# The last down projection of a two-layer trunk by seven products over K pairs

## The chip, the cores and the metric

The kernel runs on one core of one Trainium2 chip as one launch. Its time is the device time in microseconds of that core. The time before is the median of three runs. The profile is one further execution of the same program, recorded by the profiler; its span runs from the first to the last instruction.

## The reference, cut to what matters

A trunk of two layers over 1024 prompt frames and 32 sample frames, model width 1024, in float32. Layer 0 has a retention mixer, layer 1 a gated linear attention; after each mixer comes a ConvFFN of width 2816, and at the end one RMS norm. The change lies in the ConvFFN of layer 1 and the final norm.

```python
def conv_ffn(h, conv_state, w_up, conv_w, conv_b, w_down):
    u = h @ w_up
    ...
    gate, val = jnp.split(c, 2, axis=-1)
    return (jax.nn.silu(gate) * val) @ w_down, ext[:, T:]

def trunk(...):
    for i in range(DEPTH):
        ...
        h = rmsnorm(x, norm_ffn[i])
        y, cs = conv_ffn(h, conv_states[i], ffn_w_up[i], ffn_conv_w[i], ffn_conv_b[i], ffn_w_down[i])
        x = x + y
    return rmsnorm(x, norm_final), ...
```

## The kernel before

Activations lie transposed: 128 features in the partitions, the 1056 frames (prompt and sample) in the columns. To keep float32 accuracy with the fp32r form that TensorE takes, each operand is split into a high part (a cast by ScalarE) and a low part (a subtraction by VectorE), and each product is three matmuls: high x high, high x low, low x high. PE is TensorE, DVE VectorE, ACT ScalarE, POOL GpSimd, SP the engine that issues most transfers.

**The up projection** (`ffn_up` with `seven`) already uses seven products in place of eight: the 1024 input features are halved, the two output tiles of one f (its gate tile and its value tile) are one side of a 2 x 2 block product, and pairs of column quarters of 264 columns the other. `ORD = (1, 2, 6, 5, 7, 4, 3)` is the order of the products, s (0 or 1) is the column half. Each product is four K tiles x three matmuls of 264 columns (L436, L440, L441). Three PSUM banks, a, b and c, hold the sums of one (f, s): products 1, 6 and 7 build up in a, 2 and later 4 use b, 5 and 3 build up in c. After products 1, 6 and 7 ACT copies the bank (`snap`, L415); after 2, 7, 4 and 3 DVE adds copy and bank into the row buffer u (`put`, L1607). Sums of weights are made on DVE (L373, L387 and neighbours). There are ten weight tiles in a ring, of which one f takes seven, so the last tiles for f + 1 come free only with the last products of f. The stage runs over 22 f; the sequence of the products of both halves is written out in `seq`, with s = 1 three and a half products behind s = 0.

After the last product of an f, `conv(f)` applies the causal convolution (per half one ACT pass, L1633, and two DVE passes, L1634 and L1635, over 1058 columns), silu on ACT (L213), the product of gate and value on DVE (L1638), and two stores of the row h into `scr_h` in DRAM.

**The last down projection** is a `Down` of 22 K tiles. It goes over the columns in three chunks (384, 384 and 288). For each chunk and K tile the weight tile w_down (128 x 1024) is loaded and split (L110), unless it was kept from the chunk before, the rows of h are loaded and split (L1483, L1484), and 8 x 3 matmuls (L1519, L1520, L1521) add into eight PSUM banks, one for each output tile. At the end of a chunk DVE adds each bank to the residual row (L1881), ACT squares it and scales it by the norm's weight. `rms_row` (L231 to L250) sums the squares over partitions with a matmul by ones and makes the inverse root (Ln, Exp, and one correction step). The scaled rows (L1902) are stored to `o_y`. For the first two chunks norm and scaling run beside the matmuls of the next chunk; for the third they follow the last matmul.

The order of the instructions on each engine is laid down at build time by a planner that takes what is ready, older instructions first; each engine then runs its queue in that order. `order(a, b)` puts a behind b. Tile pools make an instruction wait for the release of its buffer.

Buffers that the change touches: `XA`, `XB` and `XH` hold the split inputs of the up projection (28 areas of 4 x 264 columns), `AR` the rows u and c and the residual, `HR` the copies.

## Time and profile before

| | |
|---|---|
| median of 3 runs | 2813.46 us (2811.8 to 2814.3) |
| profiled execution | 2813.36 us, its span 2811.6 us, granted clock 0.998 |
| last up projection | about 2093 to 2544 us of the span |
| last down projection | 2544 to 2800.5 us |
| last matmul of it to the end of the span | 11.1 us |
| all DMA over the span | 371.10 MB, mean 132 GB/s |

Lines of the profile read as line of code, engine, operation, what is written from what, count, then busy time in us and the mean of one in ns, then the idle time of that engine just before and what ended it. PE's busy time comes from overlapping instructions: a matmul of 264 columns is listed with 284 ns, but the next one begins after less than half of that, so stages are compared by count and length, not by the sum of durations.

### The profile page before, as it was taken

The page shows a single profiled execution, that of the slowest core. Times are in us where ns is not written, and L with a number is a line of the kernel's source. Part 1 is how long each engine was busy: PE and PEld are TensorE (multiplying, and loading weights), DVE is VectorE, ACT ScalarE, POOL GpSimd, SP SyncE. Part 2 cuts the span into 40 slices and gives each one's busy share as a digit, 9 for nine tenths or more (in the row PEclk, how much of TensorE's full clock was granted, in tenths as well). Part 3 has the DMA queues.
Part 4 walks back from the last instruction along what each step waited for, and adds up shares of the span by engine and source line. Part 5 has one row for each costly group of instructions (what it writes and reads, how often), then busy time and mean ns, then how long its engine had stood idle before and what let it go on. Part 6 is the DMA issues. An engine that isn't in the chain of part 4 may idle for free.

```text
span 2811.6 us, 53490 instructions
## 1 busy us (share of the span) xinstructions
PE 2781.7 (99%) x21692; PEld 2695.0 (96%) x21692; DVE 1904.8 (68%) x3214; ACT 1337.6 (48%) x2409; POOL 311.3 (11%) x576
## 2 busy tenths in 40 slices
PE   9999999999999999999999999999999999999998
PEld 9999988888999999999999999999999999999998
DVE  7876666676457877777555576775378777775545
ACT  7544354454445444444444466653354444444444
POOL 0000000000122211111000032210132111110000
PEclk9999999999999999999999999999999999999999
DMA  6333455554875222222755501116532222227544
GB/s 239 94 113 100 148 148 151 139 150 124 284 240 182 77 84 77 78 82 84 264 185 168 168 30 53 53 45 212 187 108 80 73 85 76 84 75 253 190 150 148
DMA packets 220472, 371.10 MB, mean 132 GB/s; under 512 B 60672, under 2 KB 155008, under 8 KB 216896
## 3 DMA queue, kind: packets, MB, share of 16 engines
q1 hardware_dynamic: 212928, 330.36, 36.9%
q0 software_dynamic: 6736, 36.72, 3.9%
q8 instruction: 170, 2.79, 0.4%
q14 instruction: 78, 0.64, 0.1%
q10 hardware_dynamic: 560, 0.59, 0.1%
HBM read 275.68 MB, written 91.93 MB: 131 GB/s over the span
## 4 chain that ended last, share of the span: by engine, by line
PE 84%; DVE 7%; ACT 3%; POOL 2%; issue 2%; DMA 1%; SPq 0%; DVEq 0%; ACTq 0%; POOLq 0%
PE pu L441 13%; PE pu L436 13%; PE pu L440 13%; PE pd L1519 8%; PE pd L1521 8%; PE pd L1520 8%; PE psv L270 2%; PE psv L271 2%; PE psv L272 2%; POOL x L1122 2%; PE pg L133 1%; PE pg L134 1%; PE pg L135 1%; PE pj L885 1%; DMA raw<-w_ro 1%
## 5 line engine op out<-in xcount | busy, mean ns | idle before, releaser
L110 DVE TENSOR_TENSOR wlo<-raw,whi 128x1024 fp32r<-128x1024 f32 x188 | 234.5, 1250 | 221.6 <-ACT whi L110 211.1
L110 ACT CAST whi<-raw 128x1024 fp32r<-128x1024 f32 x188 | 196.9, 1050 | 282.1 <-PE pd L1520 210.0
L1519 PE MATMUL pd<-hh,whi 128*128 128x384 f32 (+1 forms) x880 | 285.0, 324 | 0.0
L1520 PE MATMUL pd<-hl,whi 128*128 128x384 f32 (+1 forms) x880 | 284.3, 323 | 0.1
L1521 PE MATMUL pd<-hh,wlo 128*128 128x384 f32 (+1 forms) x880 | 283.9, 323 | 0.0
L415 ACT COPY HR<-pu 128x264 f32<-128x264 f32 x264 | 98.7, 375 | 311.8 <-PE pu L441 305.5
L441 PE MATMUL pu<-XA,wgl 128*128 128x264 f32 x752 | 213.4, 284 | 0.0
L436 PE MATMUL pu<-XA,wgh 128*128 128x264 f32 x752 | 212.8, 283 | 0.0
L440 PE MATMUL pu<-XA,wgh 128*128 128x264 f32 x752 | 212.5, 283 | 0.0
L1520 PEld LDWEIGHTS pd<-hl,whi 128*128 128x128 f32 x880 | 165.7, 188 | 0.9 <-DVE hl L1484 0.4
L1634 DVE SCALAR_TENSOR_TENSOR AR<-AR,cw 128x1058 f32<-128x1058 f32 x88 | 115.8, 1318 | 74.7 <-ACT AR L1633 74.6
L1519 PEld LDWEIGHTS pd<-hh,whi 128*128 128x128 f32 x880 | 165.7, 188 | 0.4
L1521 PEld LDWEIGHTS pd<-hh,wlo 128*128 128x128 f32 x880 | 165.7, 188 | 0.1
L373 DVE TENSOR_TENSOR wtl<-rv,wth 128x1024 fp32r<-128x1024 f32 x58 | 71.0, 1224 | 113.5 <-ACT wth L372 113.4
L1607 DVE TENSOR_TENSOR AR<-HR,pu 128x264 f32<-128x264 f32 (+2 forms) x440 | 144.3, 368 | 4.6 <-PE pu L441 4.6
L436 PEld LDWEIGHTS pu<-XA,wgh 128*128 128x128 f32 x752 | 141.2, 188 | 0.3 <-ACT wgh L372 0.3
L440 PEld LDWEIGHTS pu<-XA,wgh 128*128 128x128 f32 x752 | 141.2, 188 | 0.0
L441 PEld LDWEIGHTS pu<-XA,wgl 128*128 128x128 f32 x752 | 141.1, 188 | 0.0
L436 PE MATMUL pu<-XA,wsh 128*128 128x264 f32 x464 | 132.6, 286 | 2.4 <-ACT HR L415 1.3
L441 PE MATMUL pu<-XA,wtl 128*128 128x264 f32 x464 | 131.9, 284 | 0.0
L441 PE MATMUL pu<-XA,wsl 128*128 128x264 f32 x464 | 131.8, 284 | 0.0
L436 PE MATMUL pu<-XA,wth 128*128 128x264 f32 x464 | 131.6, 284 | 0.0
(503 smaller groups left out, 9625.1 us busy)
## 6 DMA issues: line engine op xcount, KB each, us to landing
raw<-w_down SPq DMA_DIRECT2D x120, 512.0 KB, 3.7
rg<-w_up SPq DMA_DIRECT2D x44, 512.0 KB, 3.6
rv<-w_up SPq DMA_DIRECT2D x44, 512.0 KB, 3.6
scr_h<-AR SPq DMA_DIRECT2D x44, 512.0 KB, 2.6
raw<-w_ro SPq DMA_DIRECT2D x39, 512.0 KB, 5.7
XH<-scr_hr POOLq DMA_DIRECT2D x16, 1056.0 KB, 7.1
HR<-scr_h SPq DMA_DIRECT2D x84, 192.0 KB, 3.9
scr_hr<-hl SPq DMA_DIRECT2D x20, 512.0 KB, 4.2
```

The source lines that it names most:

```text
L110: ins = S.copy(hi, raw), V.tensor_tensor(lo, raw, hi.bitcast(F32), op=ALU.subtract)
L270: PE.matmul(ps, ah, hi, start=kt == 0, stop=False)
L373: split_end[0] = split_last[0] = V.tensor_tensor(l_, src, h.bitcast(F32), op=ALU.subtract)
L415: ins = S.copy(t, b)
L436: mm = PE.matmul(ps, wh[:, k], x[:, 0, kt], start=m in (1, 2, 4, 5) and kt == 0, stop=False, skip_group_check=True)
L440: PE.matmul(ps, wh[:, k], x[:, 1, kt], start=False, stop=False, skip_group_check=True)
L441: mm = PE.matmul(ps, wl[:, k], x[:, 0, kt], start=False, stop=kt == 3, skip_group_check=True)
L1519: PE.matmul(o, w[0][:, k], h[0][:, :n], start=i == 0, stop=False)
L1520: PE.matmul(o, w[0][:, k], h[1][:, :n], start=False, stop=False)
L1521: self.last_mm = PE.matmul(o, w[1][:, k], h[0][:, :n], start=False, stop=i == nk - 1)
L1607: last_put[0] = V.tensor_tensor(u[:, d:d + n], t[:, o:o + n], b[:, o:o + n], op=op)
L1634: V.scalar_tensor_tensor(cj, uj[:, 1:T + 3], cw[:, nt, 1:2], cj, op0=ALU.mult, op1=ALU.add)
```

## The change

It replaces the three chunks of the last down projection by the seven-product form. The 22 K tiles become 11 pairs, the 8 output tiles 4 pairs, the columns two halves s of two quarters each.

- `pair_sums`, in place of L1638 and the two stores: after the convolution of an odd f the product rows of both f of a pair are combined into the seven right-hand operands (four subtractions of 528 columns, in two steps that are called at later products), and the seven are stored to `scr_h7`, each when it is made.
- `Down7` runs over 14 windows n. Window n holds the K pairs n - 3 to n, so one to four of them (`win`), and the output pair (n + 1) % 4. Every K pair so meets each of the four output pairs in four successive windows. Per window there are seven products for each s, of one to four K pairs x three matmuls of 264 columns, s = 0 and s = 1 in turn. The weights of a window are loaded as two tiles, combined and split as in the up projection (`weights`). The operands of a K pair are loaded and split once (`load_x`); four K pairs stay in `XA`, `XB` and `XH`.
- In windows 0 to 9 the bank sums go by ACT and DVE into blocks in `AR` and `HR` (five for the first output tile, two for the second), and POOL adds each block to the residual in `scr_x` by an adding transfer (`add`).
- The last four windows (10 to 13, output pairs 3, 0, 1, 2) complete an output pair each: the row pair with all that was added is fetched (`fetch`) and the banks are added into it (`settle`). `squares` gathers the sums of squares; with the last pair each quarter's norm is made and all four pairs are scaled and stored.
- `early` brings the first two K pairs and the weights of windows 0 and 1 in during the last f of the up projection. `final_phase` goes. `HR` is one area larger.

```diff
-    def ffn_up(l, X, fc, sm):
+    NP = NF // 2
+    class Down7:
...
+            self.win = [list(range(max(0, n - 3), min(n, NP - 1) + 1)) for n in range(NP + 3)]
...
+            self.blocks = [[HR[:, o * b:o * b + b] for o in range(3)] + [AR[:, o * b:o * b + b] for o in (8, 9)],
+                           [AR[:, o * b:o * b + b] for o in (10, 11)]]
+            self.SS = [HR[:, s * b:s * b + b] for s in range(2)]
+            self.sq = [HR[:, 4 * TH + j * TH:5 * TH + j * TH] for j in range(3)]
+            self.nsq = 0

+        def load_x(self, k, i, n=1):
+            reg, j = self.at[7 * (k % 4) + i]
+            v = reg[:, j * 4 * TH:(j + n) * 4 * TH].rearrange("p (m j u) -> p m j u", m=n, j=2)
+            hi, lo, raw = v[:, :, 0], v[:, :, 1], v[:, :, 1].bitcast(F32)
+            nc.sync.dma_start(raw, io["scr_h7"][k, :, i:i + n].rearrange("p m s t -> p m (s t)"))
+            for m in range(n):
+                self.X[k, ORD[i + m]] = v[:, m].rearrange("p j (s t) -> p j s t", s=2)
+            def split():
+                S.copy(hi, raw)
+                V.tensor_tensor(lo, raw, hi.bitcast(F32), op=ALU.subtract)
+            return split
+        def weights(self, n):
+            h = len(self.win[n]) * P
+            a, b = slice(0, h), slice(h, 2 * h)
+            rg, rv = raw_tile(f"dg{uid()}"), raw_tile(f"dv{uid()}")
+            for j, r in enumerate((rg, rv)):
+                o = self.offs[n] + j * 2 * h * P
+                nc.sync.dma_start(r[:, :2 * h], io["w_down7"][o:o + 2 * h * P].rearrange("(p c) -> p c", p=P))
+            def split(src, name):
+                hi, lo = w_tile(f"{name}h{uid()}"), w_tile(f"{name}l{uid()}")
+                S.copy(hi[:, :2 * h], src[:, :2 * h])
+                V.tensor_tensor(lo[:, :2 * h], src[:, :2 * h], hi[:, :2 * h].bitcast(F32), op=ALU.subtract)
+                return [(hi[:, c], lo[:, c]) for c in (a, b)]
+            w = self.W[n] = {}
+            w[1], w[2] = split(rg, "dwg")
+            V.tensor_tensor(rv[:, a], rv[:, a], rv[:, b], op=ALU.add)
+            V.tensor_tensor(rg[:, a], rv[:, a], rg[:, a], op=ALU.subtract)
+            V.tensor_tensor(rg[:, b], rg[:, b], rg[:, a], op=ALU.subtract)
+            v = w_tile(f"dwv{uid()}")
+            S.copy(v[:, a], rv[:, b])
+            V.tensor_tensor(v[:, b], rv[:, b], v[:, a].bitcast(F32), op=ALU.subtract)
+            w[4] = v[:, a], v[:, b]
+            V.tensor_tensor(rv[:, b], rv[:, b], rg[:, a], op=ALU.subtract)
+            w[6], w[3] = split(rg, "dws")
+            w[5], w[7] = split(rv, "dwt")
+        def block(self, j):
+            ring = self.blocks[j]
+            self.turn[j] += 1
+            return ring[(self.turn[j] - 1) % len(ring)].rearrange("p (b t) -> p b t", b=2)
+        def product(self, n, s, i):
+            m, win = ORD[i], self.win[n]
+            if i == 0:
+                self.unit[s] = {}
+            d = self.unit[s]
+            bank = {1: "a", 6: "a", 7: "a", 2: "b", 4: "b", 5: "c", 3: "c"}[m]
+            if bank not in d:
+                d[bank] = self.sm("pu")
+            ps = d[bank][:, :TH]
+            wh, wl = self.W[n][m]
+            for j, k in enumerate(win):
+                c = slice(j * P, j * P + P)
+                x = self.X[k, m][:, :, s]
+                PE.matmul(ps, wh[:, c], x[:, 0], start=m in (1, 2, 4, 5) and j == 0, stop=False,
+                          skip_group_check=True)
+                PE.matmul(ps, wh[:, c], x[:, 1], start=False, stop=False, skip_group_check=True)
+                PE.matmul(ps, wl[:, c], x[:, 0], start=False, stop=j == len(win) - 1, skip_group_check=True)
+            p, t0 = (n + 1) % 4, 2 * TH * s
+            if n >= NP - 1:
+                self.settle(p, s, m, d, ps)
+            elif m == 1:
+                d["A"] = self.block(0)
+                S.copy(d["A"][:, 0], ps)
+            elif m == 2:
+                V.tensor_tensor(d["A"][:, 0], d["A"][:, 0], ps, op=ALU.add)
+            elif m == 6:
+                S.copy(d["A"][:, 1], ps)
+            elif m == 7:
+                d["B"] = self.block(1)
+                S.copy(d["B"][:, 0], ps)
+                V.tensor_tensor(d["B"][:, 1], d["B"][:, 0], d["c"][:, :TH], op=ALU.add)
+            elif m == 4:
+                V.tensor_tensor(d["B"][:, 0], d["B"][:, 0], ps, op=ALU.subtract)
+                self.add(2 * p + 1, t0, d["B"])
+            elif m == 3:
+                V.tensor_tensor(d["A"][:, 1], d["A"][:, 1], ps, op=ALU.add)
+                self.add(2 * p, t0, d["A"])
+        def add(self, nt, t0, b):
+            G.dma_start(scr_x[:, nt, t0:t0 + 2 * TH], b.rearrange("p b t -> p (b t)"), accum_op=ALU.add)
+        def fetch(self, p):
+            o = (2 * T, 6 * T, 4 * T, 0)[p]
+            self.Y[p] = self.AR[:, o:o + 2 * T].rearrange("p (j t) -> p j t", j=2)
+            nc.sync.dma_start(self.Y[p], scr_x[:, 2 * p:2 * p + 2])
+        def settle(self, p, s, m, d, ps):
+            y = self.Y[p][:, :, 2 * TH * s:2 * TH * s + 2 * TH].rearrange("p j (b t) -> p j b t", b=2)
+            def plus(v, x, op=ALU.add):
+                V.tensor_tensor(v, v, x, op=op)
+            if m == 1 or m == 2:
+                plus(y[:, 0, 0], ps)
+            elif m == 6:
+                plus(y[:, 0, 1], ps)
+            elif m == 7:
+                plus(y[:, 1], ps.unsqueeze(1).to_broadcast([P, 2, TH]))
+                plus(y[:, 1, 1], d["c"][:, :TH])
+            elif m == 4:
+                plus(y[:, 1, 0], ps, ALU.subtract)
+                self.squares(p, s, 0)
+            elif m == 3:
+                plus(y[:, 0, 1], ps)
+                self.squares(p, s, 1)
+        def squares(self, p, s, half):
+            t0, n = 2 * TH * s + TH * half, TH
+            y = self.Y[p][:, :, t0:t0 + n]
+            ss = self.SS[s][:, TH * half:TH * half + n]
+            for j in range(2):
+                if p == 3 and j == 0:
+                    S.activation(ss, y[:, j], AF.Square)
+                    continue
+                sq = self.sq[self.nsq % 3]
+                self.nsq += 1
+                S.activation(sq, y[:, j], AF.Square)
+                (V if p == 2 else G).tensor_tensor(ss, ss, sq, op=ALU.add)
+            if p != 2:
+                for j in range(2):
+                    S.activation(y[:, j], y[:, j], AF.Copy, scale=gcol[:, 4, 2 * p + j:2 * p + j + 1])
+                return
+            rms_row([ss], t0, n, self.sm("pn"), None, False)
+            r = R[:, t0:t0 + n]
+            for q in (3, 0, 1):
+                y = self.Y[q][:, :, t0:t0 + n]
+                V.tensor_tensor(y, y, r.unsqueeze(1).to_broadcast([P, 2, n]), op=ALU.mult)
+                (S if q == 0 and s and half else nc.sync).dma_start(io["o_y"][:, 2 * q:2 * q + 2, t0:t0 + n], y)
+            y = self.Y[p][:, :, t0:t0 + n]
+            for j in range(2):
+                V.scalar_tensor_tensor(y[:, j], y[:, j], gcol[:, 4, 2 * p + j:2 * p + j + 1], r,
+                                       op0=ALU.mult, op1=ALU.mult)
+            (S if s and half else nc.sync).dma_start(io["o_y"][:, 2 * p:2 * p + 2, t0:t0 + n], y)
+        def early(self, s, i):
+            if s == 0 and i:
+                n = 1 if i == 4 else 2
+                o = 2 * i - 2
+                if i < 4:
+                    self.splits.append(self.load_x(0, o, 2))
+                elif i == 4:
+                    self.splits.append(self.load_x(0, 6))
+                    self.splits.append(self.load_x(1, 0))
+                else:
+                    self.splits.append(self.load_x(1, 2 * i - 9, 2))
+                if i == 2:
+                    self.weights(0)
+                if i > 3:
+                    later(self.splits, 1)
+            if s == 1 and i in (4, 5):
+                later(self.splits, 1)
+            if s == 1 and i == 4:
+                self.splits.append(self.load_x(1, 5, 2))
+            if s == 1 and i == 5:
+                self.weights(1)
+                later(self.splits, 1)
+        def run(self):
+            late = []
+            for n, win in enumerate(self.win):
+                for i in range(7):
+                    if n == 0 and i == 0:
+                        later(self.splits, 9)
+                    for s in range(2):
+                        self.product(n, s, i)
+                    if 2 <= n + 1 < len(self.win) and i == (2 if n > 2 else 0):
+                        self.weights(n + 1)
+                    k = n + 1
+                    if k in (2, 3):
+                        if i == 0:
+                            j = 0
+                            while j < 7:
+                                at = 7 * (k % 4) + j
+                                c = 2 if j < 6 and self.at[at][0] is self.at[at + 1][0] else 1
+                                self.splits.append(self.load_x(k, j, c))
+                                j += c
+                        elif i > 2:
+                            later(self.splits, 2)
+                    elif 3 < k < NP:
+                        late.append(self.load_x(k, i))
+                    if len(late) > 2 or late and k >= NP:
+                        late.pop(0)()
+                    if n >= NP - 2 and i == 2 and (n + 2) % 4 in (3, 0, 1, 2) and n < NP + 2:
+                        self.fetch((n + 2) % 4)
+    def ffn_up(l, X, fc, sm, he=None):
         cw, cc, cst, room = fc
+        sums_h = []
...
+            if he is not None:
+                pair_sums(f, c)
+                return
             V.tensor_tensor(c[:, 0], c[:, 0], c[:, 1], op=ALU.mult)
             nc.sync.dma_start(scr_h[f, :, 0:TP], c[:, 0, 0:TP])
             nc.sync.dma_start(scr_h[f, :, TP:T], c[:, 0, TP + 2:T + 2])
+        def pair_sums(f, c):
+            k = f // 2
+            def quarters(a):
+                return a.rearrange("p (s b t) -> p b s t", s=2, b=2)
+            def keep(m, a):
+                nc.sync.dma_start(io["scr_h7"][k, :, ORD.index(m)], a)
+            def minus(d, a, b):
+                V.tensor_tensor(d, a, b, op=ALU.subtract)
+            h = c[:, 1, 0:T] if f % 2 else he
+            V.tensor_tensor(h[:, 0:TP], c[:, 0, 0:TP], c[:, 1, 0:TP], op=ALU.mult)
+            V.tensor_tensor(h[:, TP:T], c[:, 0, TP + 2:T + 2], c[:, 1, TP + 2:T + 2], op=ALU.mult)
+            e, h, x = quarters(he), quarters(h), quarters(c[:, 0, 0:T])
+            if f % 2 == 0:
+                keep(1, e[:, 0])
+                return
+            keep(2, h[:, 0])
+            keep(3, h[:, 1])
+            def first():
+                minus(e[:, 1], e[:, 1], e[:, 0])
+                minus(x[:, 0], h[:, 1], e[:, 1])
+                keep(5, e[:, 1])
+                keep(6, x[:, 0])
+            def second():
+                minus(x[:, 1], x[:, 0], e[:, 0])
+                minus(e[:, 0], x[:, 0], h[:, 0])
+                keep(7, x[:, 1])
+                keep(4, e[:, 0])
+            sums_h.extend([first, second])
...
+                if he is not None and f == NF - 1:
+                    early(s, i)
+                if he is None and s == 0 and f == NF - 1 and i in (3, 6):
                     early(i // 6)
+                if sums_h and (s, i) in ((0, 1), (0, 4)):
+                    sums_h.pop(0)()
...
+            later(sums_h, 2)
...
-        HR = fp.tile([P, 6 * TH], F32, tag="hr", name=f"HR{l}")
+        HR = fp.tile([P, (7 if last else 6) * TH], F32, tag="hr", name=f"HR{l}")
...
-        down = Down(NF, lambda k: io["w_down"][l, k], lambda k: scr_h[k], CM, scr_x, sm, range(6, 9), 3)
-        with ex:
+        if last:
+            down = Down7(sm, [(XA, 16), (XB, 8), (XH, 4)], AR, HR)
+        else:
+            down = Down(NF, lambda k: io["w_down"][l, k], lambda k: scr_h[k], CM, scr_x, sm, range(6, 9), 3)
+        with (ExitStack() if last else ex):
...
-            sums, go = ffn_up(l, X, (cw, cc, cst, uroom), sm)
+            sums, go = ffn_up(l, X, (cw, cc, cst, uroom), sm, AR[:, 2 * (T + 2):2 * (T + 2) + T] if last else None)
...
-            with pool("db") as dp:
-                final_phase(down, second_room(dp), sm)
+            down.run()
+            ex.close()
...
-    def final_phase(down, room, sm):
...
+def _seven_down(w):
+    w = w.reshape(NF // 2, 2, P, 4, 2, P)
+    out = []
+    for n in range(NF // 2 + 3):
+        k = slice(max(0, n - 3), min(n, NF // 2 - 1) + 1)
+        for j in range(2):
+            out.append(w[k, :, :, (n + 1) % 4, j].transpose(2, 1, 0, 3).ravel())
+    return np.concatenate(out)
...
-    d["w_down"] = asc(a["ffn_w_down"].reshape(2, NF, P, D))
+    d["w_down"] = asc(a["ffn_w_down"][:1].reshape(1, NF, P, D))
+    d["w_down7"] = _seven_down(a["ffn_w_down"][1])
```

45 lines of the change are left out of this document (10 added, 35 removed).

## The prediction, made before the result was known

> **What bounds the kernel now.** I read the page's span and busy lines first, then its chain, then a table by stage, then single lines of the stages that the change touches.
>
> ```profile
> span 2811.6 us, 53490 instructions
> PE 2781.7 (99%) x21692; PEld 2695.0 (96%) x21692; DVE 1904.8 (68%) x3214; ACT 1337.6 (48%) x2409; POOL 311.3 (11%) x576
> PE 84%; DVE 7%; ACT 3%; POOL 2%; issue 2%; DMA 1%; SPq 0%; DVEq 0%; ACTq 0%; POOLq 0%
> ```
>
> PE is busy for 99% of the span and holds 84% of the chain that ended last, so a removed matmul is worth its issue interval, as long as nothing else becomes late. The stages, in a table by windows (busy time and instructions of PE, PEld, DVE, ACT, POOL; clock; DMA share; GB/s):
>
> ```profile
> 2134.00:2544.00 410.00, 410.00 (x3376) 409.66 (x3375) 315.42 (x463) 185.75 (x262) 54.78 (x139) 1.00 0.26 86
> 2544.00:2800.50 256.50, 256.50 (x1585) 255.94 (x1584) 134.51 (x177) 113.20 (x175) 11.93 (x10) 1.00 0.57 184
> 2800.50:2811.60 11.10, 1.67 (x6) 0.64 (x4) 4.64 (x9) 2.74 (x7) 0.00 (x0) 0.68 0.31 106
> ```
>
> Row one is the last up projection, already made of seven products with 264 columns: 410.0/3376 = 0.1214 us from one matmul to the next. Row two is the last down projection. Row three, 11.1 us, is what follows the last of its matmuls: last eviction, norm, scaling, stores. DVE is busy 77% of the time in the first stage and 52% in the second: the change spends some of that.
>
> **The matmuls.** Before: 22 K tiles x 8 N tiles x 3 chunks x 3 (high and low parts) = 1584 matmuls, 256.5 us. After: 11 K pairs x 4 N pairs x 7 products x 2 column halves x 3 = 1848 matmuls of 264 columns, which the up stage issues at 0.1214 us: 224.4 us. Saved: **32.1 us**. Per column both stages cost 0.460 ns (256.5 us over 528 x 1056 columns; 0.1214 us over 264), so no fixed part per matmul shows, and 264 more of them cost nothing by themselves.
>
> The Trainium skill (TensorE: Matmul & The Clock Gate, Back-to-back issue gap) gives N/2.4 + 2.5 ns per matmul; its fixed part speaks against smaller matmuls, and by it the saving would be an estimated 28.4 us. The trace disagrees on both parts (0.460 ns per column, none fixed), and the trace is used.
>
> **DVE's prices.** All further terms are DVE work, so its rows come next, and four lines of its timeline in the up stage:
>
> ```profile
> L373 DVE TENSOR_TENSOR wtl<-rv,wth 128x1024 fp32r<-128x1024 f32 x58 | 71.0, 1224 | 113.5 <-ACT wth L372 113.4
> L387 DVE TENSOR_TENSOR rg<-rv,rg 128x512 f32<-128x512 f32 x58 | 39.7, 684 | 0.2
> L1607 DVE TENSOR_TENSOR AR<-HR,pu 128x264 f32<-128x264 f32 x264 | 101.8, 424 | 2.7 <-PE pu L441 2.6
> L1638 DVE TENSOR_TENSOR AR<-AR 128x1058 f32<-128x1058 f32 x44 | 55.5, 1261 | 6.3 <-ACT AR L213 1.0
> L1634 DVE SCALAR_TENSOR_TENSOR AR<-AR,cw 128x1058 f32<-128x1058 f32 x88 | 115.8, 1318 | 74.7 <-ACT AR L1633 74.6
> 2325.65 0.68 DVE L387 TENSOR_TENSOR rg<-rv,rg 128x512 f32<-128x512 f32 x1
> 2326.26 0.39 DVE L1607 TENSOR_TENSOR AR<-HR,pu 128x232 f32<-128x232 f32 x1
> 2326.56 0.68 DVE L388 TENSOR_TENSOR rg<-rg 128x512 f32<-128x512 f32 x1
> 2327.16 0.68 DVE L401 TENSOR_TENSOR rv<-rv,rg 128x512 f32<-128x512 f32 x1
> ```
>
> From 512 to 1024 columns 0.540 us are added, 1.05 ns each. In a queue without waits the next instruction starts 0.08 us before the row's duration is over (2325.65 + 0.68 is 2326.33, the next began at 2326.26). So at pace DVE takes about 0.20 us for 128 columns, 0.34 for 256 and 264, 0.47 for 384, 0.60 for 512, 0.62 for 528, 1.14 for 1024, 1.17 for 1056 and 1.23 for a convolution step.
>
> **The up stage.** Per pair of f: two products h (1.24 each with their 32-column parts) in place of two L1638 (1.18), and four subtractions of 528 columns (2.5): +2.6 us in 40.8 us of PE time. DVE idles 23% of that stage, 9.4 us per pair, so the work is covered; without the cover it would be 2.6 x 11 = 29 us. SP issues seven stores per pair in place of four, at a DMA share of 0.26. The one buffer for c is now held until the stores of the sums have landed, and ACT, which starts the next convolution in it, has its copies of PSUM queued behind that. A store of the up stage lands in 2.6 us:
>
> ```profile
> scr_h<-AR SPq DMA_DIRECT2D x44, 512.0 KB, 2.6
> ```
>
> The next convolution comes 20 us after the last (168 matmuls), and sums and stores, 2.5 and about 3 us, fit. I take 0; bounds 0 and 3 us.
>
> **Full windows of the new stage.** Windows 3 to 10 have four K pairs, 168 matmuls, 20.4 us of PE. DVE: weights 3 x 1.14 + 5 x 0.60 = 6.4; seven splits of X, 7 x 0.62 = 4.3; eight evictions of 0.34 = 2.7; in all 13.4 us. Covered. The evictions, three copies by ACT and four operations by DVE per half, are those of the up stage.
>
> **The transition.** Windows 0, 1 and 2 have one, two and three pairs: 5.1, 10.2 and 15.3 us of PE, with nearly the work of a full window on DVE, and the convolution of f = 21 arrives when the up stage ends. DVE's load until window 1 can start: that convolution and its sums 4 x 1.23 + 1.24 + 4 x 0.62 = 8.6; the part of window 1's weights whose tiles come free only then, about 2.1; two splits of X, 2.3; window 0's evictions 2.7: 15.7 us against 5.1. Window 1: weights for window 2 (4.9), X of pair 2 (4.1), evictions (2.7): 11.7 against 10.2. Window 2: 13.2 against 15.3. How DVE's order treats this shows at the same place now:
>
> ```profile
> 2543.71 0.49 DVE L1607 TENSOR_TENSOR AR<-HR,pu 128x232 f32<-128x232 f32 x2 [0.42 <-PE pu L441]
> 2544.12 1.31 DVE L1634 SCALAR_TENSOR_TENSOR AR<-AR,cw 128x1058 f32<-128x1058 f32 x1
> ...
> 2546.18 0.91 ACT L1483 CAST hh<-HR 128x384 fp32r<-128x384 f32 x2
> ...
> 2547.72 2.56 DVE L1635 SCALAR_TENSOR_TENSOR AR<-AR,cw 128x1058 f32<-128x1058 f32 x2
> ...
> 2550.18 1.02 DVE L1484 TENSOR_TENSOR hl<-HR,hh 128x384 fp32r<-128x384 f32 x2
> ...
> 2552.26 1.26 DVE L1638 TENSOR_TENSOR AR<-AR 128x1058 f32<-128x1058 f32 x1
> 2553.43 0.55 DVE L1484 TENSOR_TENSOR hl<-HR,hh 128x384 fp32r<-128x384 f32 x1
> ```
>
> The splits L1484 were ready at 2547.1, when ACT's casts ended, and stood behind both L1635: the older convolution goes first. It ended 9.7 us after the last put began (2543.71 to 2553.4). With 2.5 us of sums behind it, window 0's evictions come some 12 us after the up stage's end. In window 0, product 4 reuses the PSUM bank of product 2 and so waits for its eviction, from 3.7 us on (ten products of 0.364). PE stands about 8 us. Such a pause costs clock, too:
>
> ```profile
> 1637.60:1641.00 3.40, 1.72 (x12) 1.72 (x13) 3.40 (x11) 2.65 (x11) 1.02 (x3) 0.92 0.02 5
> 1641.00:1644.00 3.00, 3.00 (x17) 3.00 (x16) 2.24 (x6) 0.61 (x2) 0.00 (x0) 0.52 0.00 0
> 1644.00:1648.00 4.00, 4.00 (x34) 4.00 (x33) 2.24 (x5) 2.70 (x8) 0.00 (x0) 1.00 0.00 0
> ```
>
> After PE had half idled for 3.4 us its clock was 0.52 for some 3 us, and 17 matmuls began in 3 us instead of 25: 1.5 us lost. Some of the rest overlaps; I take **9 us**. Upper bound: DVE's whole excess (10.6 + 1.5), and 1.5 for the clock, 14. Lower bound 0: pair 10 is fetched in window 9 at the earliest, so its 8.6 us could be put back, and the weights and splits worked ahead.
>
> **The tail.** The last four windows finish output tiles 6-7, 0-1, 2-3, 4-5 on a fetched residual. No column has its norm before the last window, which has 42 matmuls, 5.1 us; so the scaling of all 1056 columns lies behind it, where before two of three chunks were scaled under PE. Rows of the end now:
>
> ```profile
> 2800.48 0.46 DVE L1881 TENSOR_TENSOR AR<-AR,pd 128x288 f32<-128x288 f32 x1 [0.40 <-PE pd L1521]
> ...
> 2804.23 0.46 DVE L250 SCALAR_TENSOR_TENSOR R<-rt,R 128x288 f32<-128x288 f32 x1
> 2804.72 2.83 DVE L1902 TENSOR_TENSOR AR<-AR,R 128x576 f32<-128x576 f32 x5
> ```
>
> DVE from the last window's start: evictions 2 x (6 x 0.34 + 0.62) = 5.3. Then for each of four quarters two additions of squares 0.68, three steps of the norm 1.02, three scalings of 528 and two of 264 columns 2.54; 4.24 x 4 = 17.0. Together 22.3 us. It starts 0.5 us into the window; the chain from eviction to scaling takes 4.2 us (2800.48 to 2804.72), in which the other quarters' small steps fill about half, and evictions wait for products by turns: 2.5 us idle. DVE ends 25.3 us into the window. Before, 4.05 us lay between the last scaling's end (2807.55) and the span's end; with that, 29.4. Less the window's 5.1 us this is 24.3 us behind PE's nominal end, against 11.1: **+13 us**. The squares of window 12 are added by POOL, which doesn't hold this up:
>
> ```profile
> L158 POOL TENSOR_TENSOR ss<-ss,sq 128x264 f32<-128x264 f32 x24 | 20.4, 852 | 53.9 <-ACT sq L147 53.7
> ```
>
> Eight of 0.85 us from 8 us into that window of 10.2 end 5 us into the last one, before its own squares are due. Bounds: +10 without idle time; +17 if the 4.3 MB of output can't keep up (184 GB/s at share 0.57 is 323 GB/s at full share, 13.4 us from the first scaling on, some 11 us into the window; its landing would then add).
>
> **The adds in DRAM.** Forty transfers of 264 KB, from POOL's queue, each adding into scr_x. The trace has no adding transfer; the nearest rows are plain stores from the same queue and from SP:
>
> ```profile
> scr_x<-AR POOLq DMA_DIRECT2D x32, 264.0 KB, 6.3
> scr_x<-AR SPq DMA_DIRECT2D x16, 192.0 KB, 1.9
> L1768 POOL DMA_DIRECT2D scr_x<-AR x32 | 23.4, 731 | 47.9 <-DVE AR L1762 37.4 <-issue 10.2
> ```
>
> POOL issues one in 0.73 us, four per window: hidden. Two blocks serve the second row of outputs, one per half: a block sent after product 4 is written again at product 7 of the next window, 17 us later in full windows (20.4 less one step of 2.9 and an eviction). At 6.3 us this is free; at four times that it isn't. I take 0; the upper end is a rival.
>
> **Sum**, against the profiled execution (2813.36 us: span 2811.6 and 1.8 around it; the median 2813.46 is the same within 0.1): 2813.4 - 32.1 + 9 + 13 = **2803 us**.
>
> **Rivals.** (1) *The transition is covered.* For it: the one stretch where DVE is full now,
>
> ```profile
> 2100.00:2110.00 10.00, 9.87 (x81) 9.62 (x79) 10.00 (x11) 4.89 (x7) 2.16 (x1) 1.00 0.01 2
> ```
>
> costs PE only 0.13 us of 10. Against: there PE has products of four K tiles to run ahead with, window 0 has one. Transition 1, tail 10: 2792 us. (2) *DVE takes it all back.* Transition at 14, tail 13 to 17, up stage up to 3: 2808 to 2815 us. For it: each excess above is a plain sum of rows. Against: needs several upper ends at once. (3) *Slower: the adds land late.* The adding transfer must read what it adds to. Once landing passes 17 us, DVE's eviction of product 7 waits for its block, and product 3, which needs the bank that this eviction reads, stops PE. Each of six full or nearly full windows is longer by the landing less 17, so the gain is gone at 18.7 us; at four times 6.3 us it is 25.2 and 6 x 8.2 = 49 us lost: 2852 us. For it: no row shows this operation. Against: it takes a factor of three. That the change wouldn't do what it says can't be: the number of products is fixed by its loops.
>
> **How the numbers follow.** Forecast 0.55 (2797 to 2807), rival 1 0.15, rival 2 0.16, rival 3 0.14. 0.2% is 5.6 us, about what a measurement of this kernel tells from no change: faster means below 2807.8. Faster: 0.55 + 0.15 = 0.70. Same: rival 2 without its upper edge, 0.14. Slower: 0.14 + 0.02. The range takes the sums with all lower bounds, 2813.4 - 32.1 + 0 + 10 = 2791, and all upper bounds, + 14 + 17 + 3, 2815; it leaves out rival 3.
>
> **What the profile would show.** Right: about 1848 matmuls at 0.121 us in windows 3 to 10; PE waiting for DVE in the first 15 us of the stage and hardly anywhere else; DVE nearly full for the last 20 us, PE idle there. Wrong: POOL's adding transfers landing after 17 us and DVE waiting for them at product 7; gaps of PE inside the up stage or the full windows; a tail near 11 or beyond 30 us.

## The result and the profile after

| | before | after |
|---|---|---|
| median, 11 runs each | 2812.79 us (2810.64 to 2818.29) | 2819.78 us (2816.53 to 2822.93) |
| ratio, 95% interval | | 1.0025 [1.0016, 1.0035] |
| profiled execution, its span | 2813.36, 2811.6 us | 2821.19, 2819.4 us |

The forecast was 2803 us (2791 to 2815); the changed kernel is 7 us slower than before. The page after, with the lines that answer to those of before:

```profile
span 2819.4 us, 54440 instructions
PE 2762.1 (98%) x21954; PEld 2670.4 (95%) x21954; DVE 1989.9 (71%) x3450; ACT 1349.7 (48%) x2475; POOL 344.5 (12%) x628
PE 80%; DVE 7%; ACT 3%; DMA 3%; issue 3%; POOL 2%; SPq 0%; DVEq 0%; ACTq 0%; POOLq 0%
```

PE has 20 us less to do, yet the span is longer by 8; in the chain PE falls from 84% to 80% and DMA rises from 1% to 3%. The table by stage (busy time and instructions of PE, PEld, DVE, ACT, POOL; clock; DMA share; GB/s) says where:

```profile
2134.00:2544.00 410.00, 409.06 (x3370) 408.63 (x3368) 345.89 (x534) 190.41 (x269) 52.80 (x138) 1.00 0.33 109
2544.00:2795.60 251.60, 235.06 (x1853) 231.47 (x1853) 176.34 (x309) 116.24 (x223) 51.56 (x64) 0.98 0.67 172
2795.60:2819.40 23.80, 4.68 (x11) 1.87 (x9) 19.16 (x43) 6.85 (x18) 0.00 (x0) 0.54 0.54 182
...
2545.40:2629.10 83.70, 74.74 (x585) 73.03 (x584) 68.48 (x113) 42.65 (x75) 16.34 (x19) 0.98 0.80 198
...
2671.60:2743.60 72.00, 65.80 (x507) 64.75 (x506) 42.90 (x70) 28.20 (x51) 11.52 (x14) 0.95 0.78 212
```

The up stage is as long as before. The last projection took 251.6 us where 1848 x 0.1214 = 224.4 were due; the rest after its last matmul is 23.8 us (forecast 24.3, before 11.1). The last two rows split the loss. Row four runs from the last matmul of the up stage to the start of window 5: windows 0 to 4 are 14 x 42 = 588 matmuls, 71.4 us, so **12.3 us** are lost in the transition. Row five is windows 7, 8 and 9: 504 matmuls, 61.2 us, so **10.8 us** are lost in three windows that the prediction had as fully covered, with DVE busy 60% of the time. Windows 5, 6 and 10 to 13 lose about 3 us in all.

The clock column of the last row reads 0.95. Behind each of the two longest stands of PE in these windows (2.2 us up to 2694.2, 2.0 us up to 2739.0) the granted clock was 0.50 for 3.4 us:

```profile
2695.30:2698.70 3.40, 3.40 (x18) 3.40 (x17) 3.21 (x6) 1.11 (x2) 2.23 (x3) 0.50 1.01 274
2739.70:2743.10 3.40, 3.40 (x18) 3.40 (x17) 3.27 (x7) 1.49 (x3) 1.54 (x3) 0.50 0.53 87
```

Matmuls then began every 0.220 us in place of 0.121, which is some 1.5 us lost each time. Of the 10.8 us, PE's five stands in windows 7 to 9 are 7.0 and the two stretches of low clock about 3. The measures "transition" and "windows 7 to 9" are used for every kernel below.

Next come the waits of 2608 to 2765 us, which take in windows 7 to 9 (engine and line that waited <- who ended it: us in total, times, longest), first those of SP's queue, then those of the engines:

```profile
SPq L1707 <- DMA scr_x<-AR: 15.6, 5, 7.8
SPq L1707 <- DMA scr_x<-HR: 14.7, 4, 5.7
...
ACT XA L1627 <- DMA XA<-scr_h: 49.7, 17, 5.4
DVE XA L1628 <- ACT XA L1627: 31.2, 15, 6.0
PEld pu L1676 <- DVE AR L1693: 8.6, 8, 2.3
PE pu L1676 <- DVE AR L1693: 6.9, 6, 2.1
```

And one such place in window 7, in the timeline:

```profile
2681.61 0.32 SPq L1707 DMA_DIRECT2D AR<-scr_x  x1
2682.03 0.85 SPq L1622 DMA_DIRECT2D XA<-scr_h  x2
2683.26 0.37 SPq L1637 DMA_DIRECT2D dv<-w_down  x1
...
2687.32 1.32 ACT L1627 CAST XA<-XA 128x528 fp32r<-128x528 f32 x2 [4.79 <-DMA XA<-scr_h]
2688.54 0.37 ACT L1692 COPY AR<-pu 128x264 f32<-128x264 f32 x1
...
2687.98 1.39 DVE L1628 TENSOR_TENSOR XA<-XA 128x528 fp32r<-128x528 f32 x2 [4.75 <-ACT XA L1627]
2689.36 0.69 DVE L1647 TENSOR_TENSOR dv<-dv 128x512 f32<-128x512 f32 x1
2689.97 0.42 DVE L1693 TENSOR_TENSOR AR<-AR,pu 128x264 f32<-128x264 f32 x1
```

Read from top to bottom. The fetch (L1707) stands in SP's queue in window 7, although the code asks for it in window 9: the planner moves loads ahead. It must wait for the adding transfers of window 6, starts when the last has landed (2681.59), and only then SP issues the loads of X and weights behind it, which run beside the fetch. ACT idles 4.79 us for X, with the copy of product 7 (L1692) queued behind the cast; DVE idles 4.75 us, with the eviction L1693 behind its split. Product 3 needs the bank that L1693 reads, so PE stands.

### The profile page after: what moved, and what is told of

Same layout as the page of the kernel before. It is cut to its first block, busy times and chain, and to the rows that moved or that the text cites. A ratio compares the mean times of both kernels' runs of the same rounds, so it can differ in the third digit from the quotient of the medians.

```text
span 2819.4 us, 54440 instructions
## 1 busy us (share of the span) xinstructions
PE 2762.1 (98%) x21954; PEld 2670.4 (95%) x21954; DVE 1989.9 (71%) x3450; ACT 1349.7 (48%) x2475; POOL 344.5 (12%) x628
## 4 chain that ended last, share of the span: by engine, by line
PE 80%; DVE 7%; ACT 3%; DMA 3%; issue 3%; POOL 2%; SPq 0%; DVEq 0%; ACTq 0%; POOLq 0%
PE pu L441 13%; PE pu L436 13%; PE pu L440 13%; PE pd L1519 5%; PE pd L1521 5%; PE pd L1520 5%; PE psv L270 2%; PE psv L271 2%; PE psv L272 2%; POOL x L1122 2%; PE pu L1676 2%; PE pu L1678 2%; PE pu L1679 2%; DMA raw<-w_ro 1%; DMA XA<-scr_h 1%
## 5 line engine op out<-in xcount | busy, mean ns | idle before, releaser
L110 DVE TENSOR_TENSOR wlo<-raw,whi 128x1024 fp32r<-128x1024 f32 x131 | 163.1, 1249 | 130.6 <-ACT whi L110 122.7
L110 ACT CAST whi<-raw 128x1024 fp32r<-128x1024 f32 x131 | 136.9, 1049 | 176.0 <-PE pd L1520 110.1
L1845 DVE SCALAR_TENSOR_TENSOR AR<-AR,cw 128x1058 f32<-128x1058 f32 x88 | 115.7, 1317 | 72.9 <-ACT AR L1844 71.4
L1520 PE MATMUL pd<-hl,whi 128*128 128x384 f32 (+1 forms) x440 | 142.2, 323 | 0.1
L1519 PE MATMUL pd<-hh,whi 128*128 128x384 f32 (+1 forms) x440 | 142.2, 323 | 0.0
L1521 PE MATMUL pd<-hh,wlo 128*128 128x384 f32 (+1 forms) x440 | 141.8, 322 | 0.0
L436 PE MATMUL pu<-XA,wsh 128*128 128x264 f32 x464 | 132.5, 286 | 1.8 <-ACT HR L415 0.7
L436 PE MATMUL pu<-XA,wth 128*128 128x264 f32 x464 | 131.6, 284 | 0.0
L440 PE MATMUL pu<-XA,wsh 128*128 128x264 f32 x464 | 131.4, 283 | 0.0
L440 PE MATMUL pu<-XA,wth 128*128 128x264 f32 x464 | 131.1, 283 | 0.0
L1519 PE MATMUL pd<-XH,whi 128*128 128x264 f32 x432 | 123.6, 286 | 0.0
```

What stands on the lines that cost most here:

```text
L110: ins = S.copy(hi, raw), V.tensor_tensor(lo, raw, hi.bitcast(F32), op=ALU.subtract)
L436: mm = PE.matmul(ps, wh[:, k], x[:, 0, kt], start=m in (1, 2, 4, 5) and kt == 0, stop=False, skip_group_check=True)
L440: PE.matmul(ps, wh[:, k], x[:, 1, kt], start=False, stop=False, skip_group_check=True)
L1519: PE.matmul(o, w[0][:, k], h[0][:, :n], start=i == 0, stop=False)
L1520: PE.matmul(o, w[0][:, k], h[1][:, :n], start=False, stop=False)
L1521: self.last_mm = PE.matmul(o, w[1][:, k], h[0][:, :n], start=False, stop=i == nk - 1)
```

## Experiments

All runs stand against the kernel before on the same chip (medians 2812.2 to 2813.2 us). The up stage, the same in all but for the last convolution, ended between 2541.8 and 2549.7 us in the profiled executions, so stages are compared by their own lengths and times by medians. The columns of losses come from one profiled execution each (two of the fetch on POOL). In one table:

| kernel | median us | ratio [95%] | transition lost | windows 7-9 lost | last matmul to end |
|---|---|---|---|---|---|
| after | 2819.8 | 1.0025 [1.0016, 1.0035] | 12.3 | 10.8 | 23.8 |
| fetch on POOL | 2819.5 | 1.0019 [1.0006, 1.0031] | 9.5; 11.1 | 2.0; 8.9 | 23.3; 23.8 |
| plain store | 2803.7 | 0.9964 [0.9953, 0.9976] | 6.1 | 0.2 | 23.2 |
| four blocks | 2813.9 | 1.0004 [0.9994, 1.0013] | 10.2 | 7.5 | 23.2 |
| late convolution | 2812.8 | 0.9996 [0.9987, 1.0006] | 8.2 | 9.2 | 23.0 |
| small fetch | 2812.9 | 1.0003 [0.9993, 1.0012] | 11.4 | 4.1 | 23.3 |
| late fetch | 2808.5 | 0.9986 [0.9978, 0.9995] | 11.4 | 1.1 | 23.6 |
| late fetch, blocks, convolution | 2803.2 | 0.9968 [0.9956, 0.9979] | 7.8 | 1.7 | 23.4 |
| ... convolution held | 2802.3 | 0.9964 [0.9951, 0.9978] | 3.3 | 0.4 | 23.6 |
| ... POOL takes a third | 2803.9 | 0.9971 [0.9959, 0.9982] | 6.2 | 0.7 | 24.6 |
| ... both | 2803.5 | 0.9966 [0.9955, 0.9977] | 5.6 | 1.1 | 24.6 |
| halves | 2823.7 | 1.0032 [1.0020, 1.0045] | 11.3 | 10.1 | 14.5 |
| ... with blocks, convolution, late fetch | 2808.8 | 0.9987 [0.9979, 0.9996] | 5.3 | 1.6 | 14.4 |

**Fetch on POOL.**

```diff
-            nc.sync.dma_start(self.Y[p], scr_x[:, 2 * p:2 * p + 2])
+            G.dma_start(self.Y[p], scr_x[:, 2 * p:2 * p + 2])
```

> The four fetches of the finished residual rows are issued from POOL's queue instead of SP's; nothing else is changed. Queue theory: in windows 7, 8 and 9 the changed kernel loses 4.2, 3.0 and 3.6 us of PE time because the fetch stands on SP until an adding transfer has landed, and the loads of X and weights behind it on SP come late; with the fetch elsewhere these windows cost under 1 us each and the kernel is 8 to 11 us faster than the changed one, about 2810 us. Bandwidth theory: the X loads land late (5 to 7 us) because the adding transfers fill the DMA engines; moving the fetch changes less than 2 us, about 2819 us.

The median did not move, as the bandwidth theory has it, but the runs scatter from 2807 to 2825 us, and the profiled execution was the fastest of them. A second profiled execution of the same kernel:

> The same kernel as the one with the fetches on POOL's queue, a second look, since its profiled execution (2807.3 us) was the fastest of ten with a median of 2819.5. Theory (fetches and adds in one queue: where an add lands late, the adds behind the fetch stand, and ScalarE waits for a block of the ring of two): in an execution near 2819 us the copies of product 7 wait over 10 us in all for the landing of adds, and windows 7 to 9 lose some 10 us. Rival (the scatter lies in the up stage or ahead of it): the last stage is as long as in the first profile, 238 us from the end of the up stage to the last matmul, and the up stage ends later.

This execution took 2817.15 us. Windows 7 to 9 of the first execution, then of the second:

```profile
2667.00:2730.10 63.10, 62.52 (x506) 61.67 (x505) 42.94 (x70) 28.03 (x51) 12.30 (x16) 1.00 0.90 241
```
```profile
2669.40:2739.40 70.00, 64.00 (x505) 63.13 (x505) 40.97 (x67) 26.42 (x50) 11.98 (x15) 0.98 0.81 216
```

The scatter lies here, 6.9 us of the 9.9 between the two. SP's queue is free in both. In window 7 of the first the loads of weights and X went out at 2679.05 and 2679.47 us, just ahead of the fetch (2679.51), and landed in 3.6 and 3.8 us; in the second the fetch started first (2680.80; the loads at 2681.34 and 2681.76) and they took 5.8 and 7.3; that window lost 1.1 us in the first execution and 5.7 in the second. Window 8 shows the same (0.4 and 2.6 us lost); in window 9 the loads went first in both executions, and both lost 0.6 us or less. ACT's wait for the blocks, which the first theory named, was 7.4 us in the first execution and 15.4 in the second, but none of it lies in these windows. So the fetch costs when it runs ahead of the loads that PE needs next, also where it doesn't hold their queue.

**Plain store.** The blocks are stored over `scr_x` and not added.

```diff
-            G.dma_start(scr_x[:, nt, t0:t0 + 2 * TH], b.rearrange("p b t -> p (b t)"), accum_op=ALU.add)
+            G.dma_start(scr_x[:, nt, t0:t0 + 2 * TH], b.rearrange("p b t -> p (b t)"))
```

> The forty adding transfers become plain stores of the same blocks to the same places (the additions in DRAM are left out). Bandwidth theory: with less DMA work per block the X loads land in under 4 us and windows 5 to 9 lose under 3 us together instead of 12.6; the waits of ACT's copies for a free block (13.8 us) go, too; about 2805 us. Queue theory: landing gets shorter by some 2 us out of 6, so that each fetch holds SP less; 3 to 6 us faster than the changed kernel, 2814 to 2817 us. If the adds cost nothing by themselves: 2819 us.

16 us less, the time of the bandwidth theory, and windows 5 to 11 lose 0.1 us or less each (ACT's waits for a block fell from 13.8 to 6.4 us and did not go altogether):

```profile
2666.10:2727.50 61.40, 61.40 (x507) 61.40 (x506) 42.42 (x70) 29.42 (x51) 6.19 (x13) 1.00 0.71 242
```

The DMA queues in 2608 to 2760 us (packets, MB, share of 16 engines; then transfers, size, median us to landing) of the changed kernel and of this one:

```profile
q0 software_dynamic: 4032, 7.57, 32.0%
...
XA<-scr_h SPq DMA_DIRECT2D x25, 264.0 KB, 5.2
scr_x<-AR POOLq DMA_DIRECT2D x20, 264.0 KB, 6.0
```
```profile
q0 software_dynamic: 2026, 6.84, 11.7%
...
XA<-scr_h SPq DMA_DIRECT2D x24, 264.0 KB, 3.4
scr_x<-AR POOLq DMA_DIRECT2D x18, 264.0 KB, 3.8
```

The adding transfers hold the DMA engines for 32.0% of that time where plain stores of nearly as many bytes hold 11.7%, and land in 6.0 us in place of 3.8. The Trainium skill (DMA: Bandwidth & Descriptors, Rules for kernel authors) says that an accumulating transfer reads its destination and writes it later; no row here shows the reading itself. SP's fetches still waited 17.3 us in this kernel, at no cost to PE: the wait alone is not the price. But they started 6.0, 5.7 and 6.3 us into windows 7 to 9, where those of the changed kernel started 10.0, 9.1 and 9.7 us in. At the earlier time the same megabyte cost nothing, though the loads issued right behind it still took 4.1 to 5.6 us to land.

**Four blocks.** Two more blocks for the second row of outputs.

```diff
-                           [AR[:, o * b:o * b + b] for o in (10, 11)]]
+                           [AR[:, o * b:o * b + b] for o in (10, 11, 12, 13)]]
```

> The ring of blocks for the second output tile has four blocks instead of two. If the transition's 13.1 us come from ACT's copies of product 7, which wait 4.3, 1.8 and 5.2 us in windows 1 to 3 until an adding transfer has left its block: these waits vanish and the kernel is 3 to 6 us faster than the changed one, 2814 to 2817 us. If the transition is bound by DVE's sum of work, as the prediction had it: less than 1.5 us, about 2819 us, PE then waiting for DVE at the same places.

ACT's waits at product 7 for a block to land (13.8 us in four places, all in the short first windows) are gone, and 6 us of the time. In the profile 2.1 us of it are in the transition. Windows 7 to 9 lose 7.5 us in place of 10.8, all of it in window 9 (0.3 in place of 3.6). There the edit also moved a fetch: the two added blocks lie in `AR` where the third fetch puts its rows, and this fetch started at 2744.85 us, in window 10, in place of window 9. So part of this kernel's gain is a fetch placed later, and not the blocks.

**Late convolution.** The convolution of f = 21, its sums and the change of the activation table move from the end of the up stage to window 3.

```diff
-                if s == 1 and i == 6:
+                if s == 1 and i == 6 and not (he is not None and f == NF - 1):
                     conv(f)
...
+                    if n == 3 and i == 0:
+                        later(late_conv, 1)
```

> The convolution of f = 21 with its sums and the table load are put off to the start of window 3; everything is still computed. If DVE's work at the transition (8.6 us of it from this convolution, older than the evictions of window 0) is what stops PE: the transition loses 3 to 6 us instead of 13.1, and the kernel is 7 to 10 us faster than the changed one, about 2811 us. If blocks or loads are what is late there: within 2 us of 2819 us.

The time fell by 7.0 us, as the first theory had it; the transition lost 4 us less, but the 8.2 us that are left miss that theory's 3 to 6. Window 1 lost 0.1 us in place of 6.0 (from its first matmul to that of window 2), windows 2 and 4 lost 2.5 us more. In the changed kernel the convolution stands on DVE ahead of the evictions of product 2 (L1687), as the prediction had it:

```profile
2549.82 1.31 DVE L1845 SCALAR_TENSOR_TENSOR AR<-AR,cw 128x1058 f32<-128x1058 f32 x1
...
2553.49 2.54 DVE L1846 SCALAR_TENSOR_TENSOR AR<-AR,cw 128x1058 f32<-128x1058 f32 x2
...
2558.36 0.42 DVE L1687 TENSOR_TENSOR HR<-HR,pu 128x264 f32<-128x264 f32 x1
```

But these evictions are not what PE waited for. PE's own waits in the transition (2545.4 to 2629.1 us), then ACT's queue ahead of the longest of them:

```profile
PE pu L1676 <- DVE AR L1693: 2.6, 3, 1.0
PE pu L1676 <- ACT HR L1689: 2.6, 1, 2.6
PE pu L1676 <- ACT AR L1692: 2.4, 3, 1.2
PE pu L1676 <- ACT HR L1685: 1.3, 1, 1.3
...
2555.26 1.13 ACT L213 ACTIVATE AR<-AR 128x1058 f32<-128x1058 f32 x1
2556.41 1.28 ACT L217 ACT_TABLE_LOAD   x1
2557.70 0.38 ACT L1689 COPY HR<-pu 128x264 f32<-128x264 f32 x1
```

6.3 us are waits for copies by ACT. The longest, 2.6 us, is for a copy of product 6 (L1689) that stood behind the convolution's silu and the change of the activation table. The waits for DVE (L1693, product 7) come at 2588 us and later. The edit moves the convolution's work on both engines, so it shows what the convolution costs there, about 4 us, and not that DVE's part of it does.

**Late fetch.** The fetch stays on SP, placed behind a matmul of the window in which the code asks for it.

```diff
-            nc.sync.dma_start(self.Y[p], scr_x[:, 2 * p:2 * p + 2])
+            order(nc.sync.dma_start(self.Y[p], scr_x[:, 2 * p:2 * p + 2]), after)
```

> The fetches stay in SP's queue, but each is placed behind the matmuls of the window in which the code asks for it, some 45 us later, when the adding transfers it waits for have long landed. Theory (place in the queue): the loads of X and weights no longer stand behind a waiting fetch, windows 7 to 9 lose under 1 us each in place of 4.2, 3.0 and 3.6, the transition keeps its 13 us, and the time is 2819.8 - 10 = 2810 us, with little scatter. Rival (bandwidth): the adding transfers take the DMA engines for as long as before, loads land as late as before, windows 7 to 9 keep about 10 us, and the time stays at 2817 to 2820 us.

11.3 us less than the changed kernel, and faster than before. Windows 7 to 9, then the queue of the adding transfers in 2608 to 2760 us:

```profile
2675.00:2737.30 62.30, 62.12 (x506) 61.57 (x506) 42.48 (x70) 28.32 (x51) 11.17 (x13) 1.00 0.82 210
```
```profile
q0 software_dynamic: 4032, 7.57, 31.8%
```

The adds hold the DMA engines as long as ever, and PE hardly stands: 1.1 us lost in place of 10.8. So the adds' bandwidth alone does not cost the 10 us, nor, by the plain stores, does the early fetch alone. The loss needs both: the adds land late, so a fetch that is issued early starts late in its window, together with the loads that PE needs next and that have piled up behind it. Where nothing has piled up it costs nothing: the late fetch of window 9 also ran ahead of two loads of X (5.3 and 4.6 us to landing), but behind that window's first load of weights, and window 9 lost 0.0 us. The scatter stayed (2805 to 2815 us), against the theory.

**Small fetch.** That leaves two halves of the early fetch: the standing queue and the megabyte beside the loads.

```diff
-            nc.sync.dma_start(self.Y[p], scr_x[:, 2 * p:2 * p + 2])
+            nc.sync.dma_start(self.Y[p][:, :, 0:64], scr_x[:, 2 * p:2 * p + 2, 0:64])
```

> The changed kernel with the fetches where they were in SP's queue and with the same waits, but of each row only 64 of 1056 columns are fetched (64 KB in place of 1056 KB), so the outputs lack most of the residual. Theory A (the standing queue alone): SP still stands up to 5 us until the adds have landed, the loads behind it are still issued together and late, windows 7 to 9 still lose 8 to 11 us, the time stays near 2818 us. Theory B (the fetch's own megabyte, started when the next loads start, slows them): loads of X and weights behind the fetch land in 3.5 to 4 us in place of 5.3 to 7.3, windows 7 to 9 lose 4 us or less, the time is 2812 us or below.

Windows 7 to 9, then SP's waits in 2608 to 2765 us:

```profile
2669.10:2734.40 65.30, 62.61 (x506) 61.70 (x505) 43.10 (x71) 28.54 (x51) 11.58 (x15) 1.00 0.80 187
```
```profile
SPq L1707 <- DMA scr_x<-AR: 13.1, 2, 7.0
SPq L1707 <- DMA scr_x<-HR: 12.4, 2, 6.4
```

SP stands nearly as long as before (25.5 us against 30.3), yet windows 7 to 9 lose 4.1 us in place of 10.8, and the time is 2812.9 us, both at the edge of theory B. So about 6.7 us go with the fetch's bytes, some 3 with the standing queue, and 1 is left with the late fetch. By the medians: 6.8 and 4.4 us. About 3 of the 6.7 us are the two stretches of low clock: here PE's longest stand in these windows was 1.3 us, and the granted clock stayed at 1.00.

**Late fetch, blocks and convolution.** The late fetch, four blocks in each ring, the convolution of f = 21 in window 5 and its sums in window 6.

```diff
+                    if (n, i) in ((5, 0), (6, 0), (6, 3)):
+                        later(late_conv, 1)
```

> As the late fetch, and with it: four blocks in each of the two rings (in place of five and two), and the convolution of f = 21 in window 5 and its sums in window 6, where DVE was busy 70% of the time in the run without additions. Theory (the transition is DVE's queue and the wait of ScalarE for a block of the ring of two): the transition falls from 13 us to 5 us or less, windows 5 and 6 take the 8 us of DVE's work without loss, and the time is 2810 - 8 = 2802 us. Rival (the transition is the loads of the first windows, which share the DMA engines): it keeps 9 us or more, and the time stays at 2808 us or above.

2803.2 us, 9.6 below before: the time of the first theory, with a transition of 7.8 us, between the 5 of the theory and the 9 of the rival. The planner had put the convolution at 2590 us, into window 3, and PE stood 3.2 us there and 2.3 at 2619 us. Hence two more edits on this kernel:

```diff
                 ins = S.activation(cj, uj[:, 2:T + 4], AF.Identity, scale=cw[:, nt, 2:3], bias=cw[:, nt, 3:4])
+                if behind is not None:
+                    order(ins, behind)
```

> The kernel with late fetch, four blocks and late convolution, and in it the convolution of f = 21 is tied behind the first matmuls of window 5 (the planner had put it at 2590 us, in window 3). Theory (what is left of the transition is DVE's queue: the convolution's passes ahead of the evictions): the gaps of PE of 0.74, 2.47 and 2.25 us at 2592 to 2619 us go, and the time falls from 2803.2 to about 2799 us. Rival (those gaps are casts that wait for late loads of X): they stay, and the time is 2803 us.

The transition lost only 3.3 us, windows 5 and 6 then lost 3.7 where it had been 1.0; the median of 2802.3 us can't be told from 2803.2. (The profiled execution here was the fastest of five, that of the kernel without this edit the slowest of six.)

```diff
-                V.tensor_tensor(y, y, r.unsqueeze(1).to_broadcast([P, 2, n]), op=ALU.mult)
+                (G if q == 3 else V).tensor_tensor(y, y, r.unsqueeze(1).to_broadcast([P, 2, n]), op=ALU.mult)
```

> The kernel with late fetch, four blocks and late convolution, and in it POOL takes one of the three plain multiplications of each quarter's scaling from DVE. Theory (the tail is DVE's work): DVE loses 4 x 0.65 = 2.6 us, the tail is 21 us in place of 23.4, the time 2800.6 us. Rival (POOL, at 0.73 us for 264 columns, becomes the last, or the two engines hinder each other): the tail stays at 23 us or more, the time 2803 us or above.

The rival held: 24.6 us behind the last matmul. One quarter of the scaling with all three on DVE (changed kernel), then with one of three on POOL:

```profile
2801.10 1.94 DVE L1749 TENSOR_TENSOR AR<-AR,R 128x528 f32<-128x528 f32 x3
```
```profile
2780.92 2.30 DVE L1752 TENSOR_TENSOR AR<-AR,R 128x528 f32<-128x528 f32 x2
...
2780.74 1.30 POOL L1752 TENSOR_TENSOR AR<-AR,R 128x528 f32<-128x528 f32 x1 [6.01 <-DVE R L250]
```

DVE takes longer for two than it had taken for three. The first of the two took 1.69 us and ended 0.56 us behind POOL's (2782.04), the second took 0.69: DVE stood until POOL was done. In the other three quarters, too, the DVE instruction that met POOL's took 1.68 to 1.80 us and ended 0.56 or 0.57 us behind it. The Trainium skill (SBUF — State Buffer, SBUF: two separate sides) says that a DVE operation with two inputs in SBUF and a GpSimd operation that reads SBUF lock each other out for a whole instruction; the trace agrees. Both edits together:

> Both of these edits together: 2797 us if both theories hold and add up; 2803 us if neither does.

2803.5 us: neither adds anything that can be measured.

**Halves.** The last two windows run for s = 0, then for s = 1; their weights share tiles, since both are needed at once.

```diff
-            for n, win in enumerate(self.win):
-                for i in range(7):
+            halves = [(n, i, (0, 1)) for n in range(NP + 1) for i in range(7)]
+            halves += [(n, i, (s,)) for s in range(2) for n in (NP + 1, NP + 2) for i in range(7)]
```

> Only the order of the last two windows is changed: both windows for s = 0, then both for s = 1, so that norm and scaling of s = 0 begin 8 us before the last matmul. Theory (the tail is DVE's work behind the last products, 11.3 us of scaling, half of which now fits under PE): from the last matmul to the end 14 to 17 us in place of 23.8, the time 2819.8 - 8 = 2812 us. Rival (the tail is the chain of norm, store and landing, the same for whichever half is last): 21 us or more, the time 2817 us or above.

The tail fell to 14.5 us, as the theory had it, but the time rose by 3.9: the last two windows lost 12.9 us in place of 1.0. By windows:

```profile
2780.00:2807.50 27.50, 18.81 (x126) 17.00 (x125) 21.83 (x49) 13.20 (x33) 10.36 (x12) 0.94 0.24 80
2807.50:2822.00 14.50, 2.38 (x7) 0.91 (x5) 9.46 (x20) 3.57 (x9) 0.00 (x0) 0.56 0.43 149
```

And by the timeline, between the evictions L1724:

```profile
2795.51 0.89 DVE L1764 SCALAR_TENSOR_TENSOR AR<-AR,gcol,R 128x264 f32<-128x264 f32 x2
2796.32 0.42 DVE L249 SCALAR_TENSOR_TENSOR rt<-rt,rm 128x264 f32<-128x264 f32 x1
2796.66 0.42 DVE L1724 TENSOR_TENSOR AR<-AR,pu 128x264 f32<-128x264 f32 x1
```

The scaling of s = 0 stood in DVE's queue ahead of the evictions that s = 1's products wait for: PE waited 7.4 us in these two windows for L1724, 3.0 of it behind the second quarter's scaling. DVE's work was moved, not covered.

> The late fetch, the four blocks, the late convolution and the order of halves together, all of the computation kept. If the three losses are independent the sum is 2819.8 - 10 - 8 - 8 = 2794 us, below the kernel before by 19 us. If one shared cause (the DMA engines' load from the adding transfers) stands behind them, what one edit frees is lost in the next place and the time stays at 2803 us or above.

2808.8 us, and 5.6 slower than without the halves: the three do not add up to 2794, and the halves are a loss in both kernels. The other gains add only in part: late fetch, four blocks and late convolution gave 11.3, 5.9 and 7.0 us each by itself and 16.6 together. One thing that they share is the fetch of window 9, which the four blocks had moved, too; whether that is all stays open.

## Why the prediction was wrong

**Matmuls, right.** 1848 matmuls were issued at the up stage's pace wherever nothing stood in the way: 504 in 61.4 us in the kernel with plain stores, 0.122 us each. The 32.1 us were there to be had.

**Up stage, right.** Forecast 0, bounds 0 to 3. Its last matmul came 1.4 us behind the cut at 2544.0 us that the prediction used; in the other kernels, whose up stage differs by its last convolution at most, it came from 2.2 us ahead of that cut to 5.7 behind it.

**Full windows, wrong; this is the step that failed.** "Covered" rested on 13.4 us of DVE work in 20.4 us of PE time. That sum is about right (DVE was busy 14.3 us per window in windows 7 to 9), but it says nothing of when the inputs of that work arrive. Windows 5 to 9 lost 12.5 us with DVE busy 62%. The prediction's own sign of being wrong, gaps of PE inside the full windows, is what came.

**Adds in DRAM, wrong in the same place.** "I take 0" weighed their landing against the reuse of a block after 17 us, and that held: 6.0 us, with no wait for a block in a full window. What the step left out is the other reader of what they write, the fetch: it stands in SP's in-order queue between the loads, is bound to the landing of the adds, and brings a megabyte when it starts. The prediction gave the fetch neither a place nor a price. That it waits for the adds and shares SP's queue with the loads could be read from the change; that the planner puts it two windows ahead of the code's place was seen only in the trace. With the fetch late, 9.7 of the 10.8 us of windows 7 to 9 are gone.

**Transition, inside its bounds, but by another wait.** Forecast 9, bounds 0 to 14, measured 12.3. The convolution did stand ahead of the evictions of product 2, but PE did not stand 8 us for them: its longest waits were for copies by ACT, behind the convolution's passes there and behind the change of the activation table, which the sum for DVE left out. Also not counted were ACT's waits for a block of the ring of two in the short windows, where a block comes round sooner than in 17 us; four blocks took 2.1 us off. Without the additions in DRAM the transition is 6.1 us, so about half of it belongs to them. That the forecast came so near is partly luck. The clock did fall to 0.50 once there, for 3.4 us; the prediction's 1.5 us for such a pause fits the size here, though its own count (17 matmuls in place of 25) gives 1.0.

**Tail, right.** Forecast 13, measured 23.8 - 11.1 = 12.7 us, DVE busy 19.16 of the 23.80 us.

**The rivals.** The slower one had the sign, the source (adding transfers) and the product at which PE stops (3, behind the eviction of 7), but not the mechanism: it needed a landing above 17 us.

The sum with what was measured: 2813.4 - 32.1 + 12.3 + 12.5 + 1.2 (windows 10 to 13) + 1.4 (up stage) + 12.7 = 2821.4, against 2821.2 profiled. With the fetch late, 2808.5 us is inside the range; in that profile the transition is 2.4 us above its forecast, and windows 5 to 13 lose 4.1 us where nothing was forecast. How the waits for blocks, the convolution on ACT and the loads share the transition was not separated.

## What to carry to other kernels

A transfer that waits for another transfer's landing is a wait in an in-order queue: list what stands behind it there, and place it (here with an explicit order) where its data are long in DRAM and its bytes meet no load that the next products need. An engine that is busy 60% of a stage covers its work only if the inputs arrive in time, so price loads by when they are issued and what runs beside them. Work taken out of a tail is won only if it stands behind, not ahead of, what the last matmuls wait for.

## What the runs showed of the hardware

An adding transfer of 264 KB held the DMA engines about 2.5 times as long per byte as a plain store (32.0% for 7.57 MB against 11.7% for 6.84 MB) and landed in 6.0 us in place of 3.8. A multiplication of 528 columns with both inputs in SBUF took DVE 0.70 us alone; while POOL ran the same, two took 2.30 us. Behind stands of PE of 2.2 and 2.0 us the granted clock was 0.50 for 3.4 us, and matmuls of 264 columns began every 0.220 us in place of 0.121.
